# A decoder trunk on one core: decay exponents laid out by transfers through device memory instead of by products

## The chip, the core and the metric

One core of a Trainium2 chip. The time is device time of one execution of the whole program in microseconds (us). TensorE multiplies, VectorE and ScalarE work element by element, GpSimd hardly appears, and SyncE (SP) issues the transfers (DMAs), in order. A DMA runs on the core's 16 DMA engines.

## What is computed

Two pre-norm residual layers on 256 tokens of width 2048, all in f32: layer 0 mixes tokens with a Mamba-2 state space scan (SSD), layer 1 with a gated linear recurrence; each is followed by a SwiGLU block and a gated embedding, and the end is an RMS norm. The change is in the SSD scan (64 heads of 64 channels in 8 groups, two chunks of 128 tokens), in the norms and in the last block:

```python
a_cs = jnp.cumsum(a, axis=-1)                       # a = dt * A, per head, inside a chunk
seg = a_cs[..., :, None] - a_cs[..., None, :]
decay_in = jnp.exp(jnp.where(causal, seg, -jnp.inf))
cb = jnp.einsum("bclgn,bcsgn->bcgls", cm, bm)       # scores, per group
y_diag = jnp.einsum("bcgls,bgrcls,bcsgrp->bclgrp", cb, decay_in, x)
...
y = x32 * lax.rsqrt(jnp.mean(x32 * x32, axis=-1, keepdims=True) + RMS_EPS)   # rms_norm
...
h = h + ple_gate * (p[i].astype(h.dtype) @ w_ple_up[i])                      # end of a layer
```

The kernel does not carry a state from the first chunk to the second. It forms the products of all three pairs of chunks that causality leaves (first with first, first with second, second with second), 3 times 128 columns for a head.

## The kernel before, in words

Activations lie with channels on partitions and 256 tokens along the row. An f32 product is split: a weight tile is cast to a rounded part hi (ScalarE, L235) and a rest lo (VectorE, L236), and so is the activation. `panel` (L239) multiplies 16 or more k-tiles into four banks of 128 channels: per weight one product of hi with both parts of the activation (512 columns, L258) and one of lo with the rounded part (256 columns, L256). It takes four k-tiles at a time: 16 products with hi, then 16 with lo. After them the halves of a bank are added (`total`: ScalarE L152, VectorE L155).

Weight tiles of 512 KB (two k-tiles) come by DMA into five buffers (`raw`, L227), and there are four buffers each for hi and lo. A load is issued when VectorE has read the tile five places before. Small work is written as generators: `panel` advances those in `post` and `side` between its products, and a scheduler then orders each engine's instructions; that order is fixed when the program is built.

In the SSD layer, `dt_part` (L390) forms the step sizes and their running sums per head (`cs`: chunk 0, chunk 1, chunk 1 plus the total of chunk 0), split into rounded part and rest on two halves of the partitions (`csr`). `group(g, ts)` (L427) does the 8 heads of a group as side work of the panel after its own: convolution and SiLU (L341 to L375), scores `cm` (L436 to L439), transposes of x (L446), then for each head `decays`: a product of identity and mask (L460), a product that spreads the head's row of sums over all partitions (L462), two exponentials with the partition's own sum as bias (through `table`, L98), and a multiply with the scores (L467). `outputs` (L471) multiplies two pairs of heads with x (L479, L481). Panels 8 to 15 of `w_ssd_in` feed the eight groups.

`rstd` (L174) sums squares over partitions by products with ones (L183), forms 1/sqrt on VectorE, and spreads it over partitions: a diagonal tile `dg` (L207), two products with ones (L212). It runs 14 times beside the panels and once at the end. The last panel (`apart`) multiplies its last four k-tiles bank by bank, so that the banks end one after another; `gate` (L688) scales a block, takes the sigmoid, adds to h, and squares for the last norm. At the end h is multiplied by the norm's row and stored (L750, L751).

Of the kernel before, what the change touches and what calls it, by code (L numbers as in the profile page):

```python
# [11 lines left out]
F32 = mybir.dt.float32  # L12
# [5 lines left out]
P = 128  # L18
T = 256
# [23 lines left out]
class Trunk:  # L43
# [7 lines left out]
    def __init__(self, ctx, tc):  # L51
# [8 lines left out]
        self.ssd = pool("ssd", 2)  # L60
        self.ps = pool("ps", 8, space=bass.MemoryType.PSUM)
# [8 lines left out]
        self.identr = c.tile([P, P], F32R, name="identr")  # L70
        nc.vector.tensor_copy(self.identr, self.ident)
        self.sel = c.tile([P, 64], F32R, name="sel")
        nc.vector.tensor_tensor(self.sel, self.ident[:, :64], self.ident[:, 64:], ALU.add)
# [4 lines left out]

        mask = self.act.tile([P, 256], F32, name="mask", tag="a")
        nc.gpsimd.memset(mask, 0.0)  # L80
        for o in (0, P):
            nc.gpsimd.affine_select(
                out=mask[:, o:o + P], in_=mask[:, o:o + P],
                compare_op=ALU.is_ge, fill=-1e30, base=0, pattern=[[1, P]], channel_multiplier=-1)
        self.mask = c.tile([P, 256], F32R, name="maskr")
        nc.vector.tensor_copy(self.mask, mask)
# [87 lines left out]
    def rstd(self, acc, n, out, wait=4, last=False):  # L174
# [64 lines left out]
    def panel(self, w, xs, pump=1.4, kt=KG, nb=NB, pre=None, post=True, apart=False):  # L239
# [5 lines left out]

        nc = self.nc
# [118 lines left out]
    def ssd_mixer(self, w_dt, w_in, w_out, load):  # L365
# [5 lines left out]

        def conv_silu(j, t, out):
# [17 lines left out]
        def dt_part(t):  # L390
# [10 lines left out]
            cs = self.act.tile([P, 384], F32, name="cs", tag="a")  # L401

            for c in range(2):
                nc.vector.tensor_tensor_scan(cs[:, c * P:(c + 1) * P], self.ones, adt[:, c * P:(c + 1) * P],
                                             0.0, ALU.mult, ALU.add)
            nc.vector.tensor_scalar(cs[:, 256:], cs[:, P:256], cs[:, P - 1:P], None, ALU.add)
# [7 lines left out]
            for i, src in enumerate((dt[:, :P], dt[:, P:], cs[:, :P], cs[:, P:256])):  # L414
# [5 lines left out]
            self.csr, self.dts, self.ncs = csr, dts, ncs  # L420
            yield

        def of0(t):

            return t[:, :384].rearrange("p (a b) -> p a b", a=3)[:, 0:3:2, :]

        def group(g, ts):  # L427
            xs = [self.act.tile([P, 2, T], F32, name=f"xs{i}", tag="a") for i in range(2)]
            xs = [t[:, i, :] for t in xs for i in range(2)]
            for j, t in enumerate(ts):  # L430
# [5 lines left out]
            nc.tensor.matmul(of0(b), bt[:, :P], ct, start=True, stop=True, skip_group_check=True)  # L436
            nc.tensor.matmul(b[:, P:256], bt[:, P:], ct[:, P:], start=False, stop=True, skip_group_check=True)
# [15 lines left out]
            es = []  # L453

            def decays(j):

# [360 lines left out]
```

## Time and profile before

| | before |
|---|---|
| median of 3 runs | 2702.58 us (2700.83 to 2703.74) |
| profiled execution, its own time | 2702.77 us |
| its span in the profile | 2701.0 us |
| TensorE (PE) busy | 2673.1 us |
| VectorE (DVE) busy | 1826.7 us |
| ScalarE (ACT) busy | 1498.9 us |
| moved by DMA | 495.24 MB, 54.9% of 16 engines' span in the issued queue |

The span is the time between the first and the last instruction of the profiled execution; the 1.8 us between it and that execution's time lie around the program. Busy time of an engine is counted over the whole span, idle time is put down to what ended it, and "L258" is line 258 of the kernel. A busy TensorE is not a TensorE at its peak: its matmuls overlap, so the distance from start to start tells more than a duration.

### The profile page before, as it was taken

What the parts mean: (1) busy time and instruction counts of PE and PEld (TensorE: products, weight loads), DVE (VectorE), ACT (ScalarE), POOL (GpSimd) and SP (SyncE); (2) the same over time, 40 slices, a digit from 0 to 9 for tenths busy, and PEclk for the clock granted to TensorE, in tenths of its full rate; (3) what the DMA queues carried; (4) which work ended last, traced back from release to release, by engine and by line L of the source; (5) the groups of instructions that cost most, each with busy time, mean ns of one, the idle gap of its engine ahead of it and who ended that gap; (6) DMA issues with size and microseconds to landing.
All of it is one profiled execution on the core that took longest, in us unless ns stands there. A gap on an engine that the chain in (4) does not pass through costs nothing.

```text
span 2701.0 us, 40721 instructions
## 1 busy us (share of the span) xinstructions
PE 2673.1 (99%) x15488; PEld 2353.0 (87%) x15488; DVE 1826.7 (68%) x3130; ACT 1498.9 (55%) x2397; POOL 1.5 (0%) x9
## 2 busy tenths in 40 slices
PE   8999999999999999999999999999999999999997
PEld 7888888888888888888888888888888888888886
DVE  7888778865566654556665899977666545665666
ACT  7667665544454444444455678856444444444555
POOL 0000000000000000000000000000000000000000
PEclk9999999999999999999999999999999999999998
DMA  6534445555555565555555555555555555556553
GB/s 230 187 128 159 145 143 181 183 199 175 198 179 190 191 197 191 179 190 190 196 185 196 187 171 191 185 186 200 190 187 188 191 191 180 187 192 202 187 187 117
DMA packets 136708, 495.24 MB, mean 183 GB/s; under 512 B 15296, under 2 KB 15424, under 8 KB 136512
## 3 DMA queue, kind: packets, MB, share of 16 engines
q1 hardware_dynamic: 136512, 492.65, 54.9%
q8 instruction: 121, 1.98, 0.3%
q14 instruction: 75, 0.61, 0.1%
HBM read 490.49 MB, written 2.10 MB: 182 GB/s over the span
## 4 chain that ended last, share of the span: by engine, by line
PE 95%; DVE 3%; ACT 1%; issue 0%; DMA 0%; DVEq 0%; SPq 0%; ACTq 0%
PE bank L258 60%; PE bank L256 31%; DVE lo L236 1%; PE bank L479 1%; PE bank L573 1%; PE bank L462 0%; DVE t L155 0%; PE bank L446 0%; PE bank L460 0%; ACT hi L235 0%; DVE c L343 0%; PE bank L212 0%; PE bank L575 0%; PE bank L481 0%; DVE xc L343 0%
## 5 line engine op out<-in xcount | busy, mean ns | idle before, releaser
L258 PE MATMUL bank<-x,hi 128*128 128x512 f32 x7376 | 1782.2, 392 | 8.3 <-DVE x L145 7.5
L258 PEld LDWEIGHTS bank<-x,hi 128*128 128x128 f32 x7376 | 1355.3, 189 | 269.8 <-DVE x L145 8.2
L235 ACT CAST hi<-raw 128x1024 fp32r<-128x1024 f32 x930 | 973.0, 1050 | 1033.9 <-PE bank L258 967.9
L236 DVE TENSOR_TENSOR lo<-raw,hi 128x1024 fp32r<-128x1024 f32 x930 | 1104.3, 1219 | 481.4 <-issue 444.5
L256 PEld LDWEIGHTS bank<-x,lo 128*128 128x128 f32 x7376 | 951.6, 191 | 40.5 <-DVE lo L236 1.9
L256 PE MATMUL bank<-x,lo 128*128 128x256 f32 x7376 | 972.3, 283 | 1.2 <-DVE lo L236 1.0
L155 DVE TENSOR_TENSOR t<-bank,s 128x256 f32<-128x256 f32 x449 | 161.8, 417 | 296.2 <-ACT s L152 295.9
L152 ACT COPY s<-bank 128x256 f32<-128x256 f32 x497 | 160.9, 375 | 14.6 <-PE bank L575 5.4
L162 DVE TENSOR_TENSOR t<-t,r 128x256 f32<-128x256 f32 x217 | 81.8, 417 | 9.1 <-ACT r L218 9.1
L343 DVE SCALAR_TENSOR_TENSOR c<-t,vecs,c 128x255 f32<-128x255 f32 (+2 forms) x144 | 61.5, 475 | 1.0 <-ACT c L341 1.0
L98 ACT ACTIVATE e<-bank,ncs 128x256 f32<-128x256 f32 (+1 forms) x128 | 44.7, 423 | 26.5 <-PE bank L462 25.9
L144 ACT ACTIVATE x<-h,vecs 128x256 fp32r<-128x256 f32 x96 | 47.3, 501 | 15.7 <-DVE h L324 13.7
L98 ACT ACT_TABLE_LOAD x41 | 52.6, 1283 | 2.5 <-DVE c L343 1.8
L324 DVE TENSOR_TENSOR h<-h,t 128x256 f32<-128x256 f32 x144 | 53.7, 416 | 0.0
L145 DVE SCALAR_TENSOR_TENSOR x<-h,vecs,x 128x256 fp32r<-128x256 f32 x96 | 45.1, 476 | 1.6 <-ACT x L144 1.6
L172 DVE TENSOR_TENSOR acc<-acc,q 128x256 f32<-128x256 f32 x104 | 43.3, 417 | 2.1 <-ACT q L171 1.3
L171 ACT ACTIVATE q<-h 128x256 f32<-128x256 f32 x104 | 41.7, 405 | 5.0 <-DVE h L324 3.4
L98 ACT ACTIVATE sg<-t 128x256 f32<-128x256 f32 x88 | 32.4, 413 | 18.4 <-DVE t L162 18.4
L136 ACT CAST x<-t 128x256 fp32r<-128x256 f32 x88 | 31.9, 404 | 18.8 <-DVE t L665 18.8
L467 DVE TENSOR_TENSOR e<-e,cm 128x384 f32<-128x384 f32 x64 | 33.9, 553 | 11.7 <-ACT e L98 11.4
L341 ACT ACTIVATE c<-t,vecs 128x256 f32<-128x256 f32 x48 | 26.2, 592 | 13.2 <-DVE t L162 13.2
L659 DVE TENSOR_TENSOR sg<-sg,r 128x256 f32<-128x256 f32 x88 | 33.1, 418 | 0.0
(124 smaller groups left out, 717.9 us busy)
## 6 DMA issues: line engine op xcount, KB each, us to landing
raw<-in_w_ffn_in_dram SPq DMA_DIRECT2D x352, 512.0 KB, 4.5
raw<-in_w_ffn_out_dram SPq DMA_DIRECT2D x176, 512.0 KB, 4.4
raw<-in_w_ssd_in_dram SPq DMA_DIRECT2D x160, 512.0 KB, 4.4
raw<-in_w_ssd_out_dram SPq DMA_DIRECT2D x64, 512.0 KB, 4.3
raw<-in_w_ple_gate_dram SPq DMA_DIRECT2D x64, 512.0 KB, 4.2
raw<-in_w_lru_in_dram SPq DMA_DIRECT2D x64, 512.0 KB, 4.1
raw<-in_w_lru_out_dram SPq DMA_DIRECT2D x32, 512.0 KB, 4.4
raw<-in_w_ple_up_dram SPq DMA_DIRECT2D x8, 512.0 KB, 5.5
```

Of the source, the lines that this page charges most:

```text
L98: i = self.nc.scalar.activation(out, in_, func, **kw).ins
L144: nc.scalar.activation(x[:, :T], src, AF.Copy, scale=w)
L145: nc.vector.scalar_tensor_tensor(x[:, T:], src, w, x[:, :T].bitcast(F32), ALU.mult, ALU.subtract)
L152: nc.scalar.copy(s, b[:, T:])
L155: nc.vector.tensor_tensor(t, b[:, :T], s, ALU.add)
L162: self.nc.vector.tensor_tensor(t, t, r, ALU.mult)
L235: nc.scalar.copy(hi, src)
L236: nc.vector.tensor_tensor(lo, src, hi.bitcast(F32), ALU.subtract)
L256: nc.tensor.matmul(b[:, T:], wt, x[:, :T], start=False, stop=k == nk - 1, skip_group_check=True)
L258: nc.tensor.matmul(b, wt, x, start=k == 0, stop=False, skip_group_check=True)
L324: self.nc.vector.tensor_tensor(hb, hb, t, ALU.add)
L343: nc.vector.scalar_tensor_tensor(out[:, d:], t[:, :T - d], self.vec(cw, (3 - d) * ntap + i), out[:, d:], ALU.mult, ALU.add)
```

## The change

The sums are no longer split and spread by products. `dt_part` stores them in a tile in device memory, `sums` (64 heads of 640 numbers: chunk 0, chunk 1 plus the total of chunk 0, 128 times -1e30, chunk 1, 128 times -1e30). `skew(g)` copies the rows of 8 heads inside device memory to `seg[g % 2]`, once for each of the 128 partitions, each time one number further to the right, in two transfers (rows of 256 and of 128 numbers). The first 128 columns of `seg` hold -1e30, so the part left of the diagonal is masked. `group` loads four tiles `e` of two heads from there and issues the copy for the group after the next. `decays` takes the exponentials in place and multiplies two heads at once with the scores. The order of the columns is now first with first, first with second, second with second.

In `rstd` the diagonal and its products become two transposes of a broadcast column, and the loops over accumulators and halves are swapped. In the last panel the last two rounds are one of 8 k-tiles, the last bank's three products add up in the same 256 columns, and its block goes from the bank straight to the multiply by r.

```diff
@@ __init__
+        self.dram = pool("dram", 1, space=bass.MemoryType.DRAM)
...
-        self.identr = c.tile([P, P], F32R, name="identr")
-        self.sel = c.tile([P, 64], F32R, name="sel")
...
-        self.mask = c.tile([P, 256], F32R, name="maskr")
...
@@ rstd
-        for c in range(2):
-            for i, a in enumerate(acc):
+        for i, a in enumerate(acc):
+            for c in range(2):
                 nc.tensor.matmul(b[:, c:c + 1], a[:, c * P:(c + 1) * P], self.ones[:, 0:1],
...
-        dg = self.tmp.tile([P, 2, P], F32, name="dg", tag="dg", bufs=1)
-        for c in range(2):
-            nc.vector.tensor_scalar(dg[:, c, :], self.ident, cur[:, c:c + 1], None, ALU.mult)
...
-            nc.tensor.matmul(b2[:, c * P:(c + 1) * P], self.ones, dg[:, c, :],
-                             start=c == 0, stop=True, skip_group_check=True)
+            nc.tensor.transpose(b2[:, c * P:(c + 1) * P], cur[:, c:c + 1].to_broadcast([P, P]), self.ident)
@@ panel
-            if lo:
+            if apart and j == nb - 1:
+                for h in range(1 if lo else 2):
+                    nc.tensor.matmul(b[:, :T], wt, x[:, h * T:(h + 1) * T], start=k + lo + h == 0,
+                                     stop=lo == 1 and k == nk - 1, skip_group_check=True)
+            elif lo:
...
-                    if len(todo) == size or k == nk:
+                    if k == nk or len(todo) == size and not (apart and k > nk - 2 * size):
@@ ssd_mixer
+        seg = [self.dram.tile([P, 8, 512], F32, name=f"seg{i}") for i in range(2)]
+        sums = self.dram.tile([64, 640], F32, name="sums")
+        def skew(g):
+            m = seg[g % 2]
+            e = sums[g * 8:g * 8 + 8, :]
+            for o, i, n in ((0, 0, 256), (256, 384, P)):
+                nc.sync.dma_start(bass.AP(m.tensor, m.offset + o, [[8 * 512 + 1, P], [512, 8], [1, n]]),
+                                  bass.AP(e.tensor, e.offset + i, [[1, P], [640, 8], [1, n]]))
@@ dt_part
+            cs = self.act.tile([P, 512], F32, name="cs", tag="a")
+            nc.vector.memset(cs[:, 256:384], -1e30)
...
-            csr = pool.tile([P, 384], F32R, name="csr", tag="csr", bufs=1)
-            nc.scalar.copy(csr, cs)
-            nc.vector.tensor_tensor(csr[64:, :], cs[64:, :], csr[64:, :].bitcast(F32), ALU.subtract)
+            for o, i, n in ((0, 0, 512), (512, 256, 128)):
+                nc.sync.dma_start(sums[:, o:o + n], cs[:64, i:i + n])
+            for m in seg:
+                nc.sync.dma_start(m[:, :, :P], cs[:, 256:384].unsqueeze(1).to_broadcast([P, 8, P]))
+            skew(0)
+            skew(1)
@@ group
             for j, t in enumerate(ts):
                 conv_silu(g * NB + j, self.scaled(t, self.r), xs[j])
+                e = pool.tile([P, 2, 384], F32, name="e", tag="e", bufs=6)
+                nc.sync.dma_start(e, seg[g % 2][:, 2 * j:2 * j + 2, :384])
+                es.append(e)
                 yield
+            if g < 6:
+                skew(g + 2)
@@ decays
-                    rb = self.bank()
-                    nc.tensor.matmul(rb[:, :256], self.identr, self.mask, start=True, stop=False,
-                                     skip_group_check=True)
-                    nc.tensor.matmul(rb[:, :384], self.sel[:, hd:hd + 1].to_broadcast([P, P]), self.csr,
-                                     start=False, stop=True, skip_group_check=True)
-                    e = pool.tile([P, 384], F32, name="e", tag="e", bufs=8)
-                    self.table(of0(e), of0(rb), AF.Exp, bias=self.ncs[:, 0, hd:hd + 1])
-                    self.table(e[:, P:256], rb[:, P:256], AF.Exp, bias=self.ncs[:, 1, hd:hd + 1])
-                    nc.vector.tensor_tensor(e, e, cm, ALU.mult)
+                    self.table(e[:, hh, :256], e[:, hh, :256], AF.Exp, bias=self.ncs[:, 0, hd:hd + 1])
+                    self.table(e[:, hh, 256:], e[:, hh, 256:], AF.Exp, bias=self.ncs[:, 1, hd:hd + 1])
                     yield
+                nc.vector.tensor_tensor(e, e, cm.unsqueeze(1).to_broadcast([P, 2, 384]), ALU.mult)
@@ ple, gate
-                self.table(t, self.scaled(t, self.r), AF.Sigmoid)
+                if t is None:
+                    t = self.tmp.tile([P, T], F32, name="t", tag="t", bufs=7)
+                    nc.vector.tensor_tensor(t, banks[j][:, :T], self.r, ALU.mult)
+                else:
+                    self.scaled(t, self.r)
+                self.table(t, t, AF.Sigmoid)
```

The first place is SP's queue, from its loads for the SSD panels on. Before, there are only the start's loads and weights (`raw`):

```order
L718 DMA h<-in_xT_dram 128x512
L720 DMA vecs<-in_vecs_dram 128x514
L227 DMA raw<-in_w_ssd_in_dram 128x1024 x8
L227 DMA raw<-in_w_dt_dram 128x1024 x2
L227 DMA raw<-in_w_ssd_in_dram 128x1024 x144
L227 DMA raw<-in_w_ssd_out_dram 128x1024 x64
```

In the change, the place where the sums are stored and the copies of groups 0 and 1 are issued (`seg_97` and `seg_98` are the two copies' targets):

```order
L211 DMA raw<-in_w_ssd_in_dram 128x1024 x15
L410 DMA sums<-cs 64x128
L412 DMA seg_97<-cs 1024x1x128
L410 DMA sums<-cs 64x512
L412 DMA seg_98<-cs 1024x1x128
L211 DMA raw<-in_w_ssd_in_dram 128x1024
L370 DMA seg_97<-sums 128x8x256
L370 DMA seg_98<-sums 128x8x256
L370 DMA seg_97<-sums 128x8x128
L211 DMA raw<-in_w_ssd_in_dram 128x1024
L370 DMA seg_98<-sums 128x8x128
L211 DMA raw<-in_w_ssd_in_dram 128x1024 x7
```

And one later group, whose pattern repeats:

```order
L211 DMA raw<-in_w_ssd_in_dram 128x1024 x6
L434 DMA e<-seg_97 128x2x384 x2
L211 DMA raw<-in_w_ssd_in_dram 128x1024
L370 DMA seg_97<-sums 128x8x256
L211 DMA raw<-in_w_ssd_in_dram 128x1024
L434 DMA e<-seg_98 128x2x384
L370 DMA seg_97<-sums 128x8x128
L434 DMA e<-seg_98 128x2x384
L211 DMA raw<-in_w_ssd_in_dram 128x1024 x6
```

Between the weight loads there now stand four loads of `e` and two copies for each group.

The second place is TensorE from the end of group 0's transposes of x to its first output products. Before:

```order
L256 MATMUL bank<-x,lo 128x256 x4
L460 MATMUL bank<-maskr,identr 128x256
L462 MATMUL bank<-csr,sel 128x384
L256 MATMUL bank<-x,lo 128x256 x12
L460 MATMUL bank<-maskr,identr 128x256
L462 MATMUL bank<-csr,sel 128x384
L460 MATMUL bank<-maskr,identr 128x256
L462 MATMUL bank<-csr,sel 128x384
L258 MATMUL bank<-x,hi 128x512 x6
L460 MATMUL bank<-maskr,identr 128x256
L462 MATMUL bank<-csr,sel 128x384
L258 MATMUL bank<-x,hi 128x512 x6
```

In the change:

```order
L247 MATMUL bank<-x,hi 128x512 x3
L245 MATMUL bank<-x,lo 128x256 x16
L247 MATMUL bank<-x,hi 128x512 x16
L245 MATMUL bank<-x,lo 128x256 x4
L477 MATMUL bank<-e,xdt 64x256
L479 MATMUL bank<-e,xdt 64x128
```

The panel's products run through, and the output products follow them without any product for the decays.

The third place is ScalarE in a group's exponentials. Before, a stretch of group 1's:

```order
L98 ACTIVATE e<-bank,ncs 128x128
L235 CAST hi<-raw 128x1024
L98 ACTIVATE e<-bank,ncs 128x2x128
L98 ACTIVATE e<-bank,ncs 128x128
L235 CAST hi<-raw 128x1024
L98 ACTIVATE e<-bank,ncs 128x2x128
L98 ACTIVATE e<-bank,ncs 128x128
L98 ACTIVATE e<-bank,ncs 128x2x128
L98 ACTIVATE e<-bank,ncs 128x128
L235 CAST hi<-raw 128x1024 x2
```

In the change, the end of a group's row of 16:

```order
L86 ACTIVATE e<-e,ncs 128x256
L86 ACTIVATE e<-e,ncs 128x128
L86 ACTIVATE e<-e,ncs 128x256
L86 ACTIVATE e<-e,ncs 128x128
L219 CAST hi<-raw 128x1024 x4
L140 COPY s<-bank 128x256 x4
```

The weight casts, which stood between the exponentials, now stand behind them.

## Rows read from the trace of the kernel before

**Rows 1.** The page: busy time by engine, and the chain's shares by engine.
```profile
PE 2673.1 (99%) x15488; PEld 2353.0 (87%) x15488; DVE 1826.7 (68%) x3130; ACT 1498.9 (55%) x2397; POOL 1.5 (0%) x9
...
PE 95%; DVE 3%; ACT 1%; issue 0%; DMA 0%; DVEq 0%; SPq 0%; ACTq 0%
```

**Rows 2.** Windows, 284 to 314 us: busy us (x instructions) by engine, clock, DMA share.
```profile
core 0: us, PE busy (x) PEld busy (x) DVE busy (x) ACT busy (x) POOL busy (x), PEclk, DMA share, GB/s
284.00:314.00 30.00, 30.00 (x190) 25.63 (x190) 23.86 (x44) 21.30 (x41) 0.00 (x0) 1.00 0.42 141
```

**Rows 3.** Timeline of TensorE, group 2: start us, length us, engine, line, what.
```profile
194.18 3.82 PE L258 MATMUL bank<-x,hi 128*128 128x512 f32 x16
...
201.79 0.38 PE L446 MATMUL bank<-ident,xs 128*128 128x128 f32 x2
201.93 1.17 PE L258 MATMUL bank<-x,hi 128*128 128x512 f32 x4
...
205.51 0.28 PE L460 MATMUL bank<-maskr,identr 128*128 128x256 f32 x1
...
205.80 0.28 PE L460 MATMUL bank<-maskr,identr 128*128 128x256 f32 x1
...
206.10 0.76 PE L256 MATMUL bank<-x,lo 128*128 128x256 f32 x5
...
213.28 0.66 PE L479 MATMUL bank<-e,xdt 128*64 128x256 f32 x4
...
224.18 1.09 PE L258 MATMUL bank<-x,hi 128*128 128x512 f32 x4
```

**Rows 4.** Timeline of all engines, the tail.
```profile
2682.68 0.64 PE L256 MATMUL bank<-x,lo 128*128 128x256 f32 x4
...
2685.37 0.42 DVE L162 TENSOR_TENSOR t<-t,r 128x256 f32<-128x256 f32 x1
...
2687.19 0.42 ACT L168 ACTIVATE acc<-h 128x256 f32<-128x256 f32 x1 [0.55 <-DVE h L324]
...
2690.48 0.48 DVE L207 TENSOR_SCALAR dg<-ident,rs_y 128x128 f32<-128x128 f32 x2
...
2692.14 4.74 DVE L750 TENSOR_TENSOR h<-h,bank 128x256 f32<-128x256 f32 x6 [1.18 <-PE bank L212]
```

**Rows 5.** Groups by line and shape: count, busy us, mean ns.
```profile
L467 DVE TENSOR_TENSOR e<-e,cm 128x384 f32<-128x384 f32 x64 | 33.9, 553 | 11.7 <-ACT e L98 11.4
...
L462 PE MATMUL bank<-csr,sel 128*128 128x384 f32 x64 | 21.2, 338 | 0.0
...
L460 PE MATMUL bank<-maskr,identr 128*128 128x256 f32 x64 | 18.5, 289 | 0.0
...
L750 DVE TENSOR_TENSOR h<-h,bank 128x768 f32<-128x768 f32 x1 | 0.9, 948 | 0.0
```

**Rows 6.** Timeline of ScalarE, group 2's exponentials.
```profile
207.92 2.87 ACT L98 ACTIVATE e<-bank,ncs 128x256 f32<-128x256 f32 x8
```

**Rows 7.** Windows, two us of the output's stores (columns of rows 2).
```profile
2696.00:2698.00 2.00, 0.00 (x0) 0.00 (x0) 0.89 (x2) 0.00 (x0) 0.00 (x0) 0.50 0.97 392
```

**Rows 8.** DMA issues: count, KB of each, median us from issue to landing.
```profile
raw<-in_w_ssd_in_dram SPq DMA_DIRECT2D x160, 512.0 KB, 4.4
...
out_dram<-h SPq DMA_DIRECT2D x1, 128.0 KB, 1.8
```

**Rows 9.** Waits of SP's queue: us in total, times, longest.
```profile
SPq L227 <- DVE lo L236: 2174.3, 868, 12.3
```

**Rows 10.** Timeline of ScalarE before group 0.
```profile
108.68 1.05 ACT L235 CAST hi<-raw 128x1024 fp32r<-128x1024 f32 x1 [2.71 <-PE bank L258]
```

**Rows 11.** Timeline of TensorE, one norm beside a panel.
```profile
389.16 0.60 PE L212 MATMUL bank<-dg,ones 128*128 128x128 f32 x4
389.52 1.68 PE L256 MATMUL bank<-x,lo 128*128 128x256 f32 x12
```

More of the change, by code (lines that the diff above doesn't have):

```diff
@@ L77, in __init__ @@
         nc.scalar.activation(warm, self.ones[:, :1], AF.Identity)
[L79 to L84, printed above, removed]
-        self.mask = c.tile([P, 256], F32R, name="maskr")
-        nc.vector.tensor_copy(self.mask, mask)
         self.vecs = c.tile([P, NVEC], F32, name="vecs")
@@ L400, in dt_part @@
             nc.vector.tensor_scalar(adt, dt, a, None, ALU.mult)
-            cs = self.act.tile([P, 384], F32, name="cs", tag="a")
-            for c in range(2):
-                nc.vector.tensor_tensor_scan(cs[:, c * P:(c + 1) * P], self.ones, adt[:, c * P:(c + 1) * P],
+            cs = self.act.tile([P, 512], F32, name="cs", tag="a")
+            nc.vector.memset(cs[:, 256:384], -1e30)
+            for c, o in ((0, 0), (1, 384)):
+                nc.vector.tensor_tensor_scan(cs[:, o:o + P], self.ones, adt[:, c * P:(c + 1) * P],
                                              0.0, ALU.mult, ALU.add)
-            nc.vector.tensor_scalar(cs[:, 256:], cs[:, P:256], cs[:, P - 1:P], None, ALU.add)
-            csr = pool.tile([P, 384], F32R, name="csr", tag="csr", bufs=1)
-            nc.scalar.copy(csr, cs)
-            nc.vector.tensor_tensor(csr[64:, :], cs[64:, :], csr[64:, :].bitcast(F32), ALU.subtract)
+            nc.vector.tensor_scalar(cs[:, P:256], cs[:, 384:], cs[:, P - 1:P], None, ALU.add)
+            for o, i, n in ((0, 0, 512), (512, 256, 128)):
[4 more added lines that the diff above has]
+            skew(1)
             yield
@@ L413, in dt_part @@
             b = self.bank()
-            for i, src in enumerate((dt[:, :P], dt[:, P:], cs[:, :P], cs[:, P:256])):
+            for i, src in enumerate((dt[:, :P], dt[:, P:], cs[:, :P], cs[:, 384:])):
                 nc.tensor.transpose(b[:, i * P:(i + 1) * P], src, self.ident)
@@ L429, in group @@
             xs = [t[:, i, :] for t in xs for i in range(2)]
+            es = []
             for j, t in enumerate(ts):
                 conv_silu(g * NB + j, self.scaled(t, self.r), xs[j])
+                e = pool.tile([P, 2, 384], F32, name="e", tag="e", bufs=6)
+                nc.sync.dma_start(e, seg[g % 2][:, 2 * j:2 * j + 2, :384])
+                es.append(e)
                 yield
+            if g < 6:
+                skew(g + 2)
             b = self.bank()
             bt, ct = bc[g // 2][:, g % 2, :], bc[4 + g // 2][:, g % 2, :]
-            nc.tensor.matmul(of0(b), bt[:, :P], ct, start=True, stop=True, skip_group_check=True)
-            nc.tensor.matmul(b[:, P:256], bt[:, P:], ct[:, P:], start=False, stop=True, skip_group_check=True)
+            nc.tensor.matmul(b[:, :256], bt[:, :P], ct, start=True, stop=True, skip_group_check=True)
+            nc.tensor.matmul(b[:, 256:384], bt[:, P:], ct[:, P:], start=False, stop=True, skip_group_check=True)
             cm = pool.tile([P, 384], F32, name="cm", tag="cm")
@@ L475, in outputs @@
                     for hh in range(2):
-                        e = es[i * 2 + hh]
+                        e = es[i][:, hh, :]
                         ch = slice(i * P + hh * 64, i * P + hh * 64 + 64)
                         o = yb[hh * 64:hh * 64 + 64, (i - j) * T:(i - j + 1) * T]
-                        nc.tensor.matmul(o, xdt[0][:, ch], of0(e), start=i == j, stop=False,
+                        nc.tensor.matmul(o, xdt[0][:, ch], e[:, :256], start=i == j, stop=False,
                                          skip_group_check=True)
-                        nc.tensor.matmul(o[:, P:256], xdt[1][:, ch], e[:, P:256], start=False, stop=True,
+                        nc.tensor.matmul(o[:, P:256], xdt[1][:, ch], e[:, 256:], start=False, stop=True,
                                          skip_group_check=True)
@@ L702, in ple @@
             last = norm == "norm_final" and n == D // PW - 1
-            ts = self.totals(self.panel(w_gate[n], u, apart=last))
+            banks = self.panel(w_gate[n], u, apart=last)
+            ts = self.totals(banks[:NB - last]) + [None] * last
             self.post.append(gate(n, ts))
```

9 lines of the change are left out of this document (2 added, 7 removed).

## The prediction

> **What bounds the kernel now.** I read four views, from the coarse to the fine. The page's first and fourth parts come first [rows 1]: TensorE is busy for 2673.1 of 2701.0 us, and 95% of the chain that ended last is TensorE's. So a piece of TensorE's work that goes away shortens the run, unless another engine or a transfer takes its place; work of other engines counts only where TensorE ends up waiting for it. The second view is a stretch of the stage that the change is about [rows 2]: from 284 to 314 us TensorE is busy throughout at full granted clock (1.00), VectorE for 23.86 and ScalarE for 21.30 of 30 us, and the DMA engines for a share of 0.42, which is 12.6 us. All three have room. The third is TensorE in order of time over one such stretch [rows 3]: one panel with the side work of one group of 8 heads runs from 194.18 to 224.18, 30.0 us. Starts count there, not durations, since matmuls overlap. The fourth is the tail, where TensorE has ended and nothing hides anything [rows 4].
>
> **The decay products.** Each head has one product with the mask (L460) and one that spreads its row of sums over partitions (L462), 64 of each [rows 5]. Two such pairs begin at 205.51 and 205.80, and the panel goes on at 206.10 [rows 3], so a pair takes 0.295 us of TensorE's time. 64 times 0.295 is 18.9 us, all of it on the bounding engine. The order of the changed kernel has none of them: 2.4 us less in each group, whose period goes from 30.0 to 27.6 us.
>
> **What takes their place on ScalarE and VectorE.** There are still 128 exponentials, now from SBUF and without the two-piece pattern; eight of them took 2.87 us [rows 6], and I take the same. The multiply with the scores becomes one instruction of 768 elements for two heads: 948 ns by the multiply of that size in the tail, against twice 553 [rows 5], 0.6 us less for a group. VectorE then has about 23.3 of 27.6 us to do and ScalarE at most 21.3, so both stay under TensorE. What matters is the order. All 16 exponentials of a group now stand in a row on ScalarE, 5.7 us, and four weight casts wait behind them. The row begins some 13.7 us after the panel's start (207.92 [rows 6]) and ends at 19.4; the four casts are for the next panel, which begins at 27.6. I cost that at nothing, and the cover is those 8 us.
>
> The wait that is new is TensorE's for the finished decays. Its first output products of a group now stand behind 16 products of 512 and 4 of 256 of the panel's third round: by the starts in the trace without the pairs, 17.1 us after the panel's start, where they began after 19.1 us before (213.28 [rows 3]). The exponentials of the first four heads end at 13.7 + 2.9 = 16.6, and the second multiply 0.95 later, 17.5. The first two heads, ready before, keep TensorE busy for about 0.75 us, until 17.8. So the margin is 0.3 us; a weight difference on VectorE that comes first (1.2 us) would use it up. The bounds are 0 and 1.5 us a group. I take 0.1, 0.8 us for eight groups.
>
> **The transfers.** The sums now go through device memory. A group has four loads of 393 KB (the tiles e) and two copies inside device memory, of 1.05 and 0.52 MB, in pieces of 1 KB and 512 B. Eight weight tiles, 4.19 MB, cost 12.6 us of the DMA engines in a group [rows 2], 3.0 us for a MB: 4.7 us for the loads and, at the same price, 4.7 us for the two copies. With the weights that is 22.0 of 27.6 us. No row shows a copy inside device memory or so many small pieces. The bounds are: below, 4.0 us, at the 392 GB/s of the output's stretch [rows 7]; above, 28.8 us, if every 128 pieces took the 1.8 us that the smallest output transfer, 128 pieces of 1 KB, took to land [rows 8], and both copies are 1024 pieces. The upper end counts the fixed part of a transfer sixteen times, so I take 4.7, near the weights' row, and keep the upper end for the rivals. A gain is excluded: nothing was transferred there before.
>
> SP issues in order, and a copy waits there for the loads that read its target, its second half for the first. Weight loads stand behind them. Those already wait for VectorE's differences, up to 12.3 us at a time [rows 9], and a weight tile lands 4.4 us after its issue [rows 8]. In each group the waits fall into that gap, so they cost nothing as long as the first copy lands within some 10 us. Before the first group two pairs of copies stand one after another, with only two weight loads between; my estimate from the landing times above is 10 us in which SP holds weights back. The casts of that stretch waited for TensorE, by up to 2.71 us at 108.68 [rows 10], with several tiles converted ahead, so I cost this at nothing too, with about 4 us to spare.
>
> **The norm.** In 14 norms inside the run, two products with ones, of two passes each, become two transposes. A set of four passes takes 0.36 us of TensorE (389.16 to 389.52) [rows 11]; a pair of transposes takes 0.14 (201.79 to 201.93) [rows 3]. 14 times 0.22 is 3.1 us. VectorE's two multiplies by the identity go, hidden. The swapped loops over the sums move nothing where there is one accumulator.
>
> **The tail.** The last product ends at 2683.32, but the last block's multiply by r begins only at 2685.37 and its square at 2687.19, because VectorE is still on the block before [rows 4]. In the change the last round covers 8 k-tiles, so the blocks end 2.8 us apart, not 1.4, and the last one needs neither copy nor add: four steps of some 0.46 us after the product, and the square begins about 2685.4. That is 1.8 us. From the diagonal at 2690.48 to the output's multiply at 2692.14 are 1.66 us [rows 4]; without the diagonal and with half the passes I take 0.8. Sixteen more products in the last panel cost some 0.2. Together 2.5 us.
>
> **Sum.** 18.9 + 3.1 + 2.5 - 0.8 = 23.7 us. The profiled execution took 2702.77 us, 0.2 us above the median of the three runs shown; 2702.8 - 23.7 = 2679.1, so **2679 us**.
>
> **Rivals.**
> *The copies become the bound* (slower). The two copies of a group occupy the DMA engines for x us, and weights queue behind. It decides from x = 10.3 us on (27.6 - 12.6 - 4.7); the balance is at about 12. At a third of the weights' rate, x = 14.4 (half of my upper bound), six groups last 31.7 us, 1.7 more than before (+10.2); two groups without copies save 4.8, norm and tail 5.6, and the start, which holds 29 us of copies, loses about 14: 2717 us. For it: no row shows such a copy, and 128 partitions read the same few KB. Against it: there is room for twice the weights' price.
> *The copies run at half the weights' rate*: 9.4 us still fit into a group (26.7 of 27.6), but the two pairs at the start outlast their cover by about 5 us, after 0.8 of decays as above: 2684 us. The Trainium skill, "DMA: Bandwidth & Descriptors", section "Latency and other measured facts", reports copies between HBM tensors at about half their rate when rows lie 4 MiB apart, which a pad of 192 bytes did not cure. The copies' targets here have rows of 16 KB plus 4 bytes, far below that pitch, and no run here shows it yet, so its chance is small.
> *TensorE waits for the decays*: 1.5 us in each group, as the row of exponentials starts late or VectorE puts a weight difference first. 12 us are given back: 2702.8 - 24.5 + 12 = 2690 us. For it: a margin of 0.3 us. Against it: a group that waited starts its next panel later, with everything else further ahead.
> *VectorE paces the stage*: with 23.3 busy us and its waits in order the period stays at 30.0, and only norm and tail count: 2697 us. Against it: TensorE had no idle time in this stage [rows 2].
> That the change doesn't remove the products can't be: they are gone from TensorE's order.
>
> **Chances and range.** Forecast 0.56, half rate 0.04, waits for the decays 0.14, VectorE 0.10, copies as the bound 0.16. The range reaches down to 2674, for no wait at all (2678) and some us from a panel that is interrupted less often, and up to 2704, past the VectorE case and the balance point of the copies; it leaves out the copies at a third of the rate and little below 2674. A difference of 0.2%, 5.4 us, is about what a measurement of this kernel can tell. Faster by more: 0.56 + 0.04 + 0.14 + 0.03 of the VectorE case = 0.77; within: 0.07; slower: 0.16.
>
> **What would show it.** Right: panels with side work last 27.5 us, TensorE's idle time before the output products is under 0.5 us a group, casts still wait for TensorE and not for a DMA, and the DMA share in the stage is near 0.8. Wrong: casts that wait for weight loads between 95 and 115 us or in the groups, copies that take over 10 us from issue to landing, or a period that stays near 30.

## The result, and the profile after

| | before | after |
|---|---|---|
| median | 2701.85 us (4 runs, 2700.83 to 2703.74) | 2726.26 us (4 runs, 2724.04 to 2728.55) |
| ratio after to before | | 1.0089, 95% interval 1.0076 to 1.0102 |
| profiled execution: time, span | 2702.77, 2701.0 us | 2724.04, 2722.3 us |

The changed kernel is slower by 24.4 us, where 23.7 us less had been forecast. The page of the changed kernel, busy time and the chain by engine and line (before: [rows 1]):

```profile
PE 2663.2 (98%) x15346; PEld 2340.8 (86%) x15346; DVE 1817.3 (67%) x3064; ACT 1498.7 (55%) x2395; POOL 0.7 (0%) x6
...
PE 90%; DVE 4%; DMA 4%; ACT 2%; issue 1%; SPq 0%; DVEq 0%; ACTq 0%
PE bank L247 58%; PE bank L245 30%; DMA raw<-in_w_ssd_in_dram 2%; DVE lo L220 1%; DVE c L332 1%; PE bank L477 1%; ACT hi L219 1%; DMA seg<-sums 1%; DVE t L143 1%; PE bank L571 0%; DVE t L150 0%; ACT L86 0%; DMA e<-seg 0%; PE bank L479 0%; PE bank L573 0%
```

TensorE does have 142 products fewer and 10 us less busy time, yet transfers now hold 4% of the chain, and the lines are the SSD layer's weights and the copies. The same window as in [rows 2] tells it for the stage: TensorE is busy for 24.58 of 30 us and its granted clock is 0.89, while the DMA engines' share, 0.77, is near the 0.8 that had been named as a sign of a right forecast.

```profile
284.00:314.00 30.00, 24.58 (x144) 20.42 (x143) 18.77 (x32) 16.92 (x33) 0.00 (x0) 0.89 0.77 220
```

One group, in order of time. SP's queue, then ScalarE, then TensorE:

```profile
237.16 0.54 SPq L370 DMA_DIRECT2D seg<-sums  x1
237.80 0.61 SPq L211 DMA_DIRECT2D raw<-in_w_ssd_in_dram  x1
238.54 0.61 SPq L434 DMA_DIRECT2D e<-seg  x1
247.56 0.54 SPq L370 DMA_DIRECT2D seg<-sums  x1
248.51 0.39 SPq L434 DMA_DIRECT2D e<-seg  x1
249.00 12.95 SPq L211 DMA_DIRECT2D raw<-in_w_ssd_in_dram  x6
```
```profile
257.24 1.04 ACT L219 CAST hi<-raw 128x1024 fp32r<-128x1024 f32 x1 [6.06 <-DMA raw<-in_w_ssd_in_dram]
258.19 0.41 ACT L86 ACTIVATE xs<-c 128x256 f32<-128x256 f32 x1
```
```profile
252.81 1.12 PE L245 MATMUL bank<-x,lo 128*128 128x256 f32 x8
258.66 0.69 PE L452 MATMUL bank<-ident,xs 128*128 128x128 f32 x2 [4.73 <-ACT xs L86]
259.00 0.99 PE L245 MATMUL bank<-x,lo 128*128 128x256 f32 x3
259.79 5.39 PE L247 MATMUL bank<-x,hi 128*128 128x512 f32 x16
```

Read from the top. The first copy goes out at 237.16; SP issues one weight load and one load of exponents, and then stands until the first copy has landed; the second goes out 10.4 us after the first. The next weights go out from 249.00 on, behind the second copy, and the first of them has landed when the cast begins, at 257.24: 20 us after the first copy's issue. ScalarE waits 6.06 us for it. The SiLU of the last block (`xs`) stands behind that cast in ScalarE's order, TensorE's transposes wait for the SiLU, and TensorE stands still for 4.73 us. So a late weight reached TensorE by way of an activation that had nothing to do with weights.

After that TensorE's next 16 products take 5.39 us where they took 3.82 [rows 3]. The windows around the wait show why (columns of [rows 2]):

```profile
250.00:253.90 3.90, 3.90 (x27) 3.24 (x25) 3.69 (x6) 1.18 (x2) 0.00 (x0) 1.00 1.01 157
253.90:258.66 4.76, 0.03 (x2) 0.00 (x1) 0.75 (x1) 1.40 (x3) 0.00 (x0) 0.75 1.00 381
258.66:263.00 4.34, 4.34 (x13) 3.66 (x14) 3.46 (x5) 4.33 (x10) 0.00 (x0) 0.50 0.67 237
264.00:265.20 1.20, 1.20 (x8) 0.98 (x7) 0.96 (x1) 1.20 (x5) 0.00 (x0) 1.00 0.26 106
```

TensorE was busy at a granted clock of 1.00 (2.4 GHz) until it ran out of work; behind the wait it has 0.50 (1.2 GHz) up to 263.00, and 1.00 again from 264 on. So a wait costs more than its length. The DMA engines are full in this stretch: a share of 1.01 at only 157 GB/s where the second copy and the weights are in flight together, then 1.00 at 381 GB/s.

The waits over the whole run (total us, times, longest), and SP's:

```profile
ACT hi L219 <- DMA raw<-in_w_ssd_in_dram: 58.0, 14, 13.1
...
PE bank L452 <- ACT xs L86: 28.1, 7, 5.4
...
PE bank L247 <- ACT hi L219: 4.9, 2, 4.2
```
```profile
SPq L370 <- DMA seg<-sums: 61.3, 8, 9.1
```

The last line of the first fence is the start, before the first group. 28.1 + 4.9 = 33.0 us of waits, and 12.5 us by which TensorE is busier (1.57 us in the 16 products above alone, at the lower clock) than in the run below with the same 15346 instructions and hardly a wait (`e10_long_pieces`, 2650.7 us busy, 2679.25 us): together 45.5 us, and the two profiled executions (2724.04 and 2679.22 us) lie 44.8 apart.

### The profile page after: what moved, and what is told of

Its sections match the earlier page's. It is cut to its first block, busy times and chain, and to the rows that moved or that the text cites. A ratio compares the mean times of both kernels' runs of the same rounds, so it can differ in the third digit from the quotient of the medians.

```text
span 2722.3 us, 40455 instructions
## 1 busy us (share of the span) xinstructions
PE 2663.2 (98%) x15346; PEld 2340.8 (86%) x15346; DVE 1817.3 (67%) x3064; ACT 1498.7 (55%) x2395; POOL 0.7 (0%) x6
## 4 chain that ended last, share of the span: by engine, by line
PE 90%; DVE 4%; DMA 4%; ACT 2%; issue 1%; SPq 0%; DVEq 0%; ACTq 0%
PE bank L247 58%; PE bank L245 30%; DMA raw<-in_w_ssd_in_dram 2%; DVE lo L220 1%; DVE c L332 1%; PE bank L477 1%; ACT hi L219 1%; DMA seg<-sums 1%; DVE t L143 1%; PE bank L571 0%; DVE t L150 0%; ACT L86 0%; DMA e<-seg 0%; PE bank L479 0%; PE bank L573 0%
## 5 line engine op out<-in xcount | busy, mean ns | idle before, releaser
L86 ACT ACTIVATE e<-e,ncs 128x256 f32<-128x256 f32 (+1 forms) x128 | 45.3, 443 | 0.1
L452 PE MATMUL bank<-ident,xs 128*128 128x128 f32 x64 | 14.1, 306 | 28.1 <-ACT xs L86 28.1
L452 PEld LDWEIGHTS bank<-ident,xs 128*128 128x128 f32 x64 | 8.2, 148 | 33.8 <-ACT xs L86 31.8
```

Of the source, the lines that this page charges most:

```text
L86: i = self.nc.scalar.activation(out, in_, func, **kw).ins
```

## The experiments

All times are medians; before is 2702.2 to 2702.7 us in these comparisons.

### Which part of the change loses the time

**Norm and tail alone** (e5_norm_tail): the changed `rstd`, `panel` and `gate` with the SSD stage of before.

> The stage of the kernel before with the norm and the tail of the changed kernel; it computes the reference. Theory A (the copies hold weights back, and the rest of the change is worth what was forecast): norm and tail are worth 3.1 + 2.5 = 5.6 us, 2701.9 - 5.6 = 2696 us. Rival C (the loss has nothing to do with the copies, other parts of the change fall short as well): 2700 us or more.

Measured: 2697.4 us, ratio 0.9981 (0.9971 to 0.9990), so 5.3 us less (2.7 to 7.8). Rival C falls for this part. The tail in the changed kernel's timeline (to [rows 4]):

```profile
2706.26 1.12 PE L242 MATMUL bank<-x,lo 128*128 128x256 f32 x8
...
2713.75 4.74 DVE L754 TENSOR_TENSOR h<-h,bank 128x256 f32<-128x256 f32 x6 [0.84 <-PE bank L197]
```

From the end of the last product to the output's multiply are 6.37 us, where [rows 4] give 8.82.

**Copies for the first two groups only** (e6_two_copies).

```diff
-            if g < 6:
-                skew(g + 2)
```

> The changed kernel with the copies of the first two groups alone; groups 2 to 7 load the exponents of groups 0 and 1 again (with their bias), so the output is another one, but loads, exponentials and products are all there. Theory A: with no copy inside the stage TensorE no longer waits 4 to 5 us in each group, the period falls from 34.4 to about 27.6 us, and only the loss before the first group stays (some 5 us): 2701.9 - 24.5 + 5 = 2682 us. Rival C (loads, exponentials or VectorE pace the stage): the period stays above 30 us, 2700 us or more.

Measured: 2686.07 us, 0.9938 (0.9923 to 0.9953). TensorE's wait for `xs` is gone and 4.7 us of waits at the start are left. The loss sits in the copies.

**No copies at all** (e1_direct): each load spreads two rows of sums over the partitions straight from device memory, and GpSimd masks the diagonal blocks.

```diff
+                nc.sync.dma_start(e, bass.AP(r.tensor, r.offset, [[0, P], [384, 2], [1, 384]]))
+                for o in (0, 256):
+                    nc.gpsimd.affine_select(
+                        out=e[:, :, o:o + P], in_=e[:, :, o:o + P], compare_op=ALU.is_ge, fill=-1e30,
+                        base=0, pattern=[[0, 2], [1, P]], channel_multiplier=-1)
```

> The changed kernel without any copy: each load of exponents spreads two rows of sums over the partitions straight from device memory, and GpSimd writes the mask into the diagonal blocks. It computes the reference. Theory A or B (the copies are the whole loss): no weight is held back, and the time is near the forecast for the changed kernel, 2679 us, 2676 to 2685. Rival C (something else in the change costs the 24 us), or a new wait, for GpSimd's 64 mask instructions: 2695 us or more.

Measured: **2681.1 us**, 0.9919 (0.9904 to 0.9934): faster than both kernels. Its page and its waits:

```profile
PE 2648.9 (99%) x15346; PEld 2331.7 (87%) x15346; DVE 1820.5 (68%) x3063; ACT 1499.3 (56%) x2395; POOL 33.6 (1%) x70
```
```profile
ACT hi L219 <- DMA raw<-in_w_ssd_in_dram: 4.3, 4, 2.1
...
PE bank L440 <- ACT xs L86: 2.6, 6, 0.5
```

The masks cost GpSimd 33 us and nobody waits long for them. TensorE has 20.0 us less to do than in the run with norm and tail alone (2668.9 us busy): the decay products, forecast at 18.9.

**A tile for each of the two copies** (e7_apart), so that the second doesn't wait on SP for the first; each load becomes two.

```diff
+        seh = [self.dram.tile([P, 8, 256], F32, name=f"seh{i}") for i in range(2)]
...
-            for o, i, n in ((0, 0, 256), (256, 384, P)):
+            for m, r, i, n in ((seg[g % 2], 512, 0, 256), (seh[g % 2], 256, 384, P)):
```

> The changed kernel with a tile in device memory of its own for each of a group's two copies, so that the second no longer waits on SP for the first; a load of exponents becomes two. It computes the reference. Theory A1 (what hurts is SP's order: SP stands for 10 us before the second copy, with the weights behind it): the weights are issued some 10 us earlier, the period falls to about 28 us and the time to 2685 to 2695 us. Rival B (what hurts is what the copies take of the DMA engines, so that weights land late wherever they are issued): the waits on weights shrink by under 2 us a group, 2712 us or more.

Measured: 2736.18 us, 1.0125 (1.0108 to 1.0142). SP issues weights right behind the copies, and they land late all the same. A1 falls as the whole story, with a flaw in the test: the loads were doubled too, and two more stores of mask rows stand before the first group. The DMA issues (KB each, median us from issue to landing) and TensorE's wait:

```profile
seg<-sums SPq DMA_DIRECT2D x8, 1024.0 KB, 11.0
...
seh<-sums SPq DMA_DIRECT2D x8, 512.0 KB, 12.8
```
```profile
PE bank L453 <- ACT xs L86: 31.0, 8, 5.3
```

### What makes a copy slow

Three runs take the shift out of the copies, on both sides (e3_aligned), on the target's side (e11_source_shift), on the source's side (e12_target_shift):

```diff
-[[8 * 512 + 1, P], [512, 8], [1, n]]      # target
+[[8 * 512, P], [512, 8], [1, n]]
-[[1, P], [640, 8], [1, n]]                # source
+[[0, P], [640, 8], [1, n]]
```

> The changed kernel with copies whose rows are not shifted, neither in the source nor in the target (every piece begins at a multiple of 512 bytes, all 128 partitions read the same addresses); the exponential takes a constant as bias, so the exponents are neither masked nor right. Same number of pieces and bytes. Theory S (the shift by 4 bytes per partition makes the copies slow): the first copy lands in 5 to 6 us after its issue in place of 10.4, and the time falls to about 2685 us. Rival P (many small pieces from device memory to device memory are slow in themselves) or H (all partitions read the same few KB): 9 us or more from issue to landing, 2720 us or more.

> The changed kernel with copies whose source is still shifted by 4 bytes per partition, but whose target rows are not; constant bias in the exponential, so the exponents are neither masked nor right. Theory T (it is the shift of the target, the writes, that makes the copies slow): near the run with both ends aligned, 2683 to 2690 us. Rival R (it is the shift of the source, the reads): 2710 us or more.

> The changed kernel with copies whose target rows are shifted as before, but whose source is not; constant bias in the exponential, so the exponents are not right. Theory T: near the changed kernel, 2712 to 2728 us. Rival R: 2683 to 2690 us.

Measured: both aligned 2685.2 us (0.9937, 0.9923 to 0.9952), source alone shifted 2686.89 (0.9941, 0.9926 to 0.9956), target alone shifted 2727.69 (1.0088, 1.0071 to 1.0104). Reads shifted by 4 bytes cost nothing that shows in the time; the whole loss goes with the shifted target. The waits behind the aligned copies (`e3_aligned`), SP's timeline in one group, and the stage's window:

```profile
ACT hi L219 <- DMA raw<-in_w_ssd_in_dram: 14.2, 8, 4.5
...
PE bank L452 <- ACT xs L86: 3.7, 3, 2.0
```
```profile
245.72 1.25 SPq L370 DMA_DIRECT2D seg<-sums  x2
247.06 3.36 SPq L211 DMA_DIRECT2D raw<-in_w_ssd_in_dram  x1
```
```profile
284.00:314.00 30.00, 30.00 (x185) 25.26 (x184) 25.80 (x43) 23.33 (x44) 0.00 (x0) 1.00 0.71 222
```

But the timeline shows a second difference. Both copies go out together: with unshifted rows, the program no longer makes the second wait for the first. So these runs don't yet separate slow writes from SP's wait.

Sources and pieces: another row of a weight tensor for each partition, in place of the same few KB for all (e4_wide_source); and 128 long, aligned pieces in place of 1024 short ones, read from a weight tensor as well (e10_long_pieces). The cut shows the first:

```diff
-            e = sums[g * 8:g * 8 + 8, :]
+            src = w_in[g]
...
+                                  bass.AP(src.tensor, src.offset + i, [[4096, P], [512, 8], [1, n]]))
```

> The changed kernel with copies that read a weight tensor, another row of 16 KB for each partition, in place of the sums; targets are shifted as in the changed kernel. Same number of pieces and bytes; the exponents are thus other numbers, and the exponential takes a constant as bias. Theory H (the copies are slow since 128 partitions read the same few KB): the first copy lands in 5 to 6 us and the time falls to about 2685 us. Rivals P and S: 9 us or more from issue to landing, 2720 us or more.

> The changed kernel with copies of the same bytes, but 128 pieces of 8 KB and 128 of 4 KB in place of 1024 of 1 KB and 1024 of 512 B; they read a weight tensor and write unshifted rows, so the exponents are other numbers, and the exponential takes a constant as bias. Theory P (the number of pieces makes the copies slow): the first copy lands in 4 to 6 us and the time is 2680 to 2690 us. Rival M (a copy from device memory to device memory is slow by its bytes, whatever the pieces, since it reads and writes there): 9 us or more from issue to landing, 2710 us or more.

Measured: 2713.68 us (1.0044, 1.0029 to 1.0058) and 2679.25 us (0.9914, 0.9899 to 0.9929). A wide source gives back 14 of the 42 us between target shifted and both aligned; H is a part, not the cause. Long pieces land sooner still, and the copies then cost nothing that shows (the run without copies took 2681.1 us). Since this run also reads another row for each partition, it does not tell the pieces from the source. The issues, and TensorE's first transposes of two groups, four panels apart:

```profile
seg<-in_w_ssd_in_dram SPq DMA_DIRECT2D x8, 1024.0 KB, 5.9
...
seg<-in_w_ssd_in_dram SPq DMA_DIRECT2D x8, 512.0 KB, 7.5
```
```profile
170.67 0.38 PE L453 MATMUL bank<-ident,xs 128*128 128x128 f32 x2
...
280.70 0.38 PE L453 MATMUL bank<-ident,xs 128*128 128x128 f32 x2
```

110.03 us for four panels is 27.5 each, the forecast 27.6.

How large the unit is: target pieces shifted by 64, 32 and 4 bytes for each head (e13, e16, e14), rows unshifted, e.g. `[[8 * 512, P], [512 + 16, 8], [1, n]]`.

> The changed kernel with an unshifted source and a target whose pieces are shifted by 64 bytes for each head, so that every piece begins at a multiple of 64 bytes but most not at one of 512; constant bias in the exponential, so the exponents are neither masked nor right. Theory T1 (what costs is that pieces begin between multiples of some small unit such as 64 bytes): as with aligned targets, 2683 to 2690 us. Rival T2 (any departure from rows at multiples of 512 bytes costs, or overlapping pieces that must wait for each other): 2710 us or more.

> As the run with pieces shifted by 64 bytes for each head, but by 32 bytes for each head: every second head's pieces begin 32 bytes past a multiple of 64. Constant bias in the exponential, so the exponents are neither masked nor right. If the unit is 32 bytes or less: 2683 to 2690 us, as with 64. If it is 64 bytes: half the pieces are slow, 2695 to 2715 us.

> As the run with pieces shifted by 64 bytes for each head, but by 4 bytes for each head: seven of eight pieces begin 4 to 28 bytes past a multiple of 64, and nothing else differs (same form, same order of the copies). Constant bias in the exponential, so the exponents are neither masked nor right. Theory T1 (writes that begin off a small unit are slow in themselves): most of the loss of the changed kernel comes back, 2710 to 2728 us. Rival W (what costs is SP's wait of the second copy for the first, which this form doesn't have): 2683 to 2690 us.

Measured: 2685.2 us (0.9936, 0.9921 to 0.9950), 2685.85 us (0.9940, 0.9925 to 0.9955) and 2725.46 us (1.0088, 1.0073 to 1.0103). 32 bytes are as good as none; nothing between 4 and 32 bytes was run. The last run did not isolate the shift as its expectation had claimed: with 4 bytes the second copy waits for the first again.

### The wait and the shift apart

**Aligned, with the wait put back** (e15_ordered) by an overlap of 64 bytes: `((0, 0, 256), (240, 368, 144))`.

> The run with both ends aligned, but the second copy begins 64 bytes earlier and so overlaps the first: it must wait on SP until the first has landed, as in the changed kernel (its pieces are 576 bytes long). Constant bias in the exponential, so the exponents are neither masked nor right. Theory T1: an aligned first copy lands in 8 to 9 us, SP holds the weights for that long, and the time stays near 2685 us, 2683 to 2695. Rival W: 2710 us or more.

**Aligned, no wait, doubled loads** (e17_apart_aligned): the run with a tile for each copy, unshifted.

> The run with a tile for each of a group's two copies (no wait between them, twice as many loads), now with neither source nor target shifted. Constant bias in the exponential, so the exponents are neither masked nor right. If the shift alone kept that run slow (theory T1): the waits in the groups go, 2685 to 2697 us with a start that loses some more than the changed kernel's. If the doubled loads or the copies' throughput as such did: 2715 us or more.

**Shifted, no wait, loads as they were** (e18_one_copy): one copy of 1536-byte pieces, `((0, 0, 384),)`.

> The changed kernel with one copy in a group in place of two: 1024 pieces of 1536 bytes, the same bytes, shifted as before, and no second copy that waits; the third block of 128 columns is read from the wrong sums, and the exponential takes a constant as bias. Theory T1 (a shifted copy is slow by itself, by its bytes): it lands in 12 us or more and weights behind it land later still, 2710 us or more. Rival W (SP's wait for the first copy costs most): 2685 to 2695 us.

Measured: 2712.28 us (1.0038, 1.0023 to 1.0052), 2705.14 us (1.0009, 1.0000 to 1.0019), 2701.19 us (0.9998, 0.9989 to 1.0007). The first falls where rival W had put it, the other two between their theories, so neither cause alone will do. (The profiled execution of the single copy, from which its landing time below is read, took 2705.24 us, 4 us above the median.) The ordered run's issues and SP's wait, then the single copy's:

```profile
seg<-sums SPq DMA_DIRECT2D x8, 1024.0 KB, 9.0
...
seg<-sums SPq DMA_DIRECT2D x8, 576.0 KB, 7.0
```
```profile
SPq L370 <- DMA seg<-sums: 51.8, 8, 7.3
```
```profile
seg<-sums SPq DMA_DIRECT2D x8, 1536.0 KB, 13.1
```

The wait costs 27 us (2685.2 to 2712.3; the second copy is also an eighth longer). With the wait, the shift adds 13 to 15 (2725.5 in the 4-byte run, 2726.3 in the changed kernel, 2727.7 with the target alone shifted). Without it, the shift costs 31 us at doubled loads (2705.1 to 2736.2) and 16 us in a single copy (2685.2 to 2701.2). The runs fall in the order of how long a group's copies take, from the first's issue to the last's landing: the sum of the two medians where the second waits, otherwise the second's median and the 0.6 us between the issues.

| run | copies of a group | first issue to last landing | time |
|---|---|---|---|
| e10_long_pieces | aligned, 128 pieces, no wait | about 8 us | 2679.3 |
| e3_aligned | aligned, no wait | 10.4 | 2685.2 |
| e11_source_shift | source shifted, no wait | 10.9 | 2686.9 |
| e13, e16 | target shifted by 64, 32 bytes, no wait | 10.8 | 2685.2, 2685.9 |
| e18_one_copy | shifted, one copy | 13.1 | 2701.2 |
| e15_ordered | aligned, wait | 16.0 | 2712.3 |
| e4_wide_source | target shifted, wait | 16.6 | 2713.7 |
| the changed kernel | shifted, wait | 17.6 | 2726.3 |
| e12, e14 | target shifted by 4 bytes, wait | 17.7, 17.8 | 2727.7, 2725.5 |
| e17, e7 | doubled loads, no wait; aligned, shifted | 9.9, 13.4 | 2705.1, 2736.2 |

Up to about 11 us the copies cost at most 8 us in all, and beyond it some 5 to 6.5 us for each further one. That is an order among medians; no run changed the landing time alone. The two runs with doubled loads lie some 20 to 35 us above that line: twice the loads, with two more stores of mask rows at the start, cost time as well. In the aligned one of them TensorE waits 11.9 us for `xs` (3.7 in `e3_aligned`) and 4.9 us at the start.

### Two misses: the copies spread out

Four smaller pairs in a group, issued between the loads (e8_spread); then the same with three sets of tiles, so that no copy should wait (e9_spread_free).

> The changed kernel with each group's two copies cut into four pairs, one for two heads, each with a tile of its own in device memory and issued on SP between the loads of exponents, some 3 to 5 us apart. The same bytes in the same pieces. It computes the reference. Theory D (what hurts is the burst: 17 us in which no weight lands; the DMA engines have room for the copies on the whole): weights slip in between, the waits on weights go, about 2690 us or less after a start that loses some 5 us. Rival B (throughput: a group's copies occupy the transfers for some 15 us wherever they stand, which with 12.6 us of weights and 4.7 us of loads is over 27.6): the period stays at 32 us or more, 2712 us or more.

> The spread copies of the run before, now with three sets of tiles in device memory and a tile for each of the two copies of a pair, so that no copy waits on SP for a load or for the other copy; more loads and more mask rows before the first group. It computes the reference. Theory D (burst and order: with the copies in small parts between the weights, 12.6 + 4.7 us of other transfers and some 11 us of copies nearly fit into 27.6 us): a period of 28 to 29.5 us in the groups with copies, 2700 us or less with a start that loses 5 to 12 us. Rival B (the copies' throughput beside weights is as low as the 17 us of a pair suggest): 32 us or more a group, 2720 us or more.

Measured: 2751.55 us (1.0180, 1.0163 to 1.0197) and 2740.83 us (1.0139, 1.0124 to 1.0154). In the first, SP stood 69.6 us for copies and 35.4 us for loads of exponents: each small copy waited for the load before it, so the test of D was spoilt by its own waits. In the second, SP's waits before a copy shrank to some 23 us, but twelve sets of mask rows stand before the first group, and TensorE lost 30.2 us there and 23.3 in the groups:

```profile
PE bank L247 <- ACT hi L219: 30.2, 1, 30.2
...
PE bank L454 <- ACT xs L86: 23.3, 6, 7.4
```

Spreading did not help in this form; since loads were doubled too in the second, whether the burst or the copies' throughput limits here stays open.

## Why the prediction was wrong

**The step that failed** is the transfers' wait, put at nothing: "they cost nothing as long as the first copy lands within some 10 us". The condition was the right kind, and its limit nearly right: copies that had all landed 10.4 to 10.9 us after the first issue left 2685 to 2687 us. But it was set for the first copy alone. In the changed kernel that one took 10.4 us and the second, which waits for it, 7.2 more, 17.6 us together, with the weights behind both: TensorE waited 33.0 us for what came late, and ran at the lower clock behind the waits.

The price, "I take 4.7, near the weights' row", was too low as well, but would have fitted. Three groups of the changed kernel, four without a copy (`e6_two_copies`) and four with long pieces (`e10_long_pieces`), columns of [rows 2]:

```profile
224.76:328.10 103.34, 87.88 (x516) 73.92 (x516) 70.12 (x114) 63.53 (x118) 0.00 (x0) 0.92 0.73 216
```
```profile
175.97:285.66 109.69, 109.69 (x690) 93.04 (x689) 92.88 (x153) 84.77 (x157) 0.00 (x0) 1.00 0.65 211
```
```profile
170.67:280.70 110.03, 110.03 (x689) 92.89 (x688) 92.95 (x153) 84.56 (x156) 0.00 (x0) 1.00 0.81 268
```

A group without a copy occupies the DMA engines for 0.65 of 27.4 us, 17.8 us (17.3 forecast for weights and loads); one of the changed kernel for 0.73 of 34.4 us, 25.1 us. So its copies took some 7.3 us where 4.7 stood, and long pieces some 4.5. Even 25.1 us is less than the forecast period of 27.6: the room that the prediction saw was there, and the weights came too late all the same. What a transfer occupies and when it lands are two prices; for a copy of this kind no row gave either, and the second was not asked of the pair.

**What the landing was made of**, in place of one rate: small pieces and a shared source together (8 to 10.4 us for the pair, aligned), targets shifted by 4 bytes (9.0 to 10.4 for the first copy with the wait; 8.5 and 9.3 to 11.0 and 12.8 without it, at doubled loads), a source shared by 128 partitions (8.8 to 9.9 for the first copy, target shifted), and the wait between the copies (10.4 to 16.0 for the pair). The Trainium skill, "DMA: Bandwidth & Descriptors", section "How a descriptor splits into AXI transactions", lets reads that begin off a multiple of 256 bytes cost extra beats. By that the shifted source should have cost something; here its copies land 0.3 and 0.5 us later (9.1 and 10.3 against 8.8 and 9.8), and the run is 1.7 us longer, inside the intervals. The Trainium skill, "Collectives: The Full Stack", section "Rules for kernel authors", asks for the buffers of collectives to be aligned to 32 bytes, against a read-modify-write. The runs at 32 and 4 bytes agree, though these are no collectives and no run shows what the DMA engine does inside. Of the row pitch that the prediction cited nothing shows: unshifted rows of 16 KB, without any pad, gave 2679.25 us with long pieces.

**The rival that came nearest** is the copies as the bound, 2717 us at a chance of 0.16. Its sign and place were right. Its mechanism, DMA engines full on the average, was not: their share over three groups is 0.73, and 7.3 us of copies are under the 10.3 from which it was to act. In the group shown above they are full in the stretch around the wait; weights come late there, and by the table above (an estimate) the buffered tiles cover some 11 us of it. The rival at half the weights' rate had a price above the measured one, 9.4 us, and still put it at nothing in the groups, for the same reason: 2684 us. The signs named for a wrong forecast all appeared: casts that wait for weight loads, a copy over 10 us, a period of 34.4 us.

**Right**: the decay products (18.9 forecast, 20.0 by TensorE's busy time; period 27.5 us, forecast 27.6); norm and tail (5.6 forecast, 5.3 measured; the tail 2.45 of 2.5); ScalarE's row of exponentials and VectorE cost nothing (25.80 of 30 us busy in the aligned run, 23.6 for a period of 27.5, forecast 23.3); no wait for decays. Without the copies' wait the sum is right: 2679.25 us in the run with long pieces, against 2679. That it fits so closely is luck: its terms were off by up to 1.1 us, and the 0.8 us for decays did not appear.

**The start**, "about 4 us to spare": it lacked 4.9 us, for the same reason: from the first copy's issue at 92.73 to 108.22 us SP issued a single weight load, 15.5 us where 10 had been estimated.

## What to carry to other kernels

Price a transfer by a row of the same kind: ends, pieces, alignment, and which earlier transfer it must wait for in its queue; a price per byte from weight loads (4.7 us a group) stood far below what the copies took to land (8 to 17.6 us), though not so far below what they occupied (7.3). A chain of dependent copies in the queue that feeds the weights held them back for the sum of the landing times. It was paid where the buffered tiles ran out, by an engine that waited for something else in order, and once more in TensorE's clock behind the wait. Where a transfer only spreads and masks data, let the load spread it and an idle engine mask it: that version took 2681.1 us.

## What the runs showed that was not expected

A shift of 4 bytes in the target slowed copies where 32 and 64 bytes did not (2725.5 against 2685.9 and 2685.2 us, part of it by the wait that the small shift brings back), and the same shift in the source did nothing that shows in the time. A copy's access pattern also decided order: with a shift of one number for each row or each head the second copy waited for the first, 61.3 us in all on SP in the changed kernel, although they write different bytes; with shifts of 8 or 16 numbers, or none, it did not wait.
